# Matmul with row normalisation on one core: other slots for the left half of a group's result, the first streamed loads ahead of the identity matrix, and one finish moved a hook later

## The chip, the cores and the metric

The kernel runs on one core of a Trainium2 chip. The metric is the device time of one execution in microseconds (us), as the median of several runs; smaller is better. The span in a profile (first to last instruction) is about 1.8 us shorter than the device time of the same run.

Engines: PE is the tensor engine, DVE the vector engine, ACT the scalar engine, POOL the pool (GpSimd) engine, SP the engine that issues the stores and the transposing copies. "q" after an engine's name is its sequencer, which issues DMAs.

## The reference

```python
# a, b: 2048 x 2048 float32, gamma: 2048, eps = 1e-5
x = np.matmul(a, b)
rms = np.sqrt(np.mean(x ** 2, axis=-1, keepdims=True) + eps)
out = (gamma * x / rms).astype(np.float32)
```

## The kernel before

The output is made in 16 row blocks of 128 rows. Blocks 0 to 3 are made while `a` and `b` stream in (the "head"). Blocks 4 to 15 are made in six groups of two blocks, g = 2 to 7, each in two halves (j = 0: left 1024 columns, j = 1: right 1024 columns), with seven products in place of eight (Strassen-Winograd form). A product is eight matmuls of 128x128 by 128x512.

The result of one block and one half is kept in float32 in one of eight tiles ("slots"), `x_slot[0..7]`. In the profiles these are called x_95 to x_102. A slot is free again when the store of its old content has landed. Which slot a half gets is set in `x_tile`, in the order in which the halves are first asked for:

```python
def x_tile(mb, h):
    if (mb, h) not in x_half:
        n = n_x[0]
        n_x[0] += 1
        x_half[mb, h] = x_slot[n if n < 8 else (0, 4, 1, 5, 2, 6, 3, 7)[n % 8]]
    return x_half[mb, h]
```

Each group asks in the order: first block left, second block left, first block right, second block right. So with this map group 4 puts its second block's left half into slot 4, which held the second block of group 2.

The half of a group, cut to what matters. `at_hook(n)` runs other work at that place in the program; in the traces here each engine does its own instructions in program order.

```python
x11, x12, x21, x22 = (x_chunk(ra, c1), x_chunk(ra, c2), x_chunk(rb, c1), x_chunk(rb, c2))
t = x22                                            # in the second block's slot
at_hook(0)
product(g, j, 2, p2); nc.scalar.copy(out=t, in_=p2)   # ACT: first writer of the slot
last_squares(); at_hook(1)
product(g, j, 5, p5); nc.vector.tensor_tensor(out=t, in0=p5, in1=t, op=ALU.add)
at_hook(2)
product(g, j, 1, p1); # ... DVE: t = p1 - t
at_hook(3)
product(g, j, 4, p2, start=False)                  # adds onto p2: PE needs the copy above done
nc.scalar.copy(out=x21, in_=p2); square(rb, x21); # ... DVE: x11 = t + x21
at_hook(4)
product(g, j, 3, p5, start=False)
# ... cut: products 7 and 6, hooks 5 to 7
```

The work in the hooks for the left half of groups after the first (`nxt` is the first block of the next group):

```python
if g == G0 + 1:
    hook(2, finish, r3)            # group 3: block 3 is still to be finished
hook(0, row_factor, nxt)
hook(1, apply, nxt)                # ACT: 1.99 us, then a transposing copy on SP
hook(1, row_norm, nxt + 1)         # ACT: two squares of 1.06 us, a root
hook(3, row_factor, nxt + 1)
hook(3, finish, 2 * g - 2)         # first block of the group before
hook(4, apply, nxt + 1)
```

In the right half, `finish(2 * g - 1)` (second block of the group before) stands in hook 2, and in groups 2 to 5 POOL issues two loads of 1 MB in hook 0 (after that no loads are left). `finish` is: DVE sum, ACT root, DVE reciprocal, then twice a DVE scaling (1.28 us) and a store of 512 KB on SP.

Of the kernel before, what the change touches and what calls it, by code (L numbers as in the profile page):

```python
# [8 lines left out]
FP32 = mybir.dt.float32  # L9
BF16 = mybir.dt.bfloat16  # L10
# [7 lines left out]
def kernel(  # L18
# [13 lines left out]
    nc = tc.nc  # L32
    P = 128
    M, K = a.shape
    _, N = b.shape
# [4 lines left out]
    CH = 512  # L40
# [4 lines left out]
    G0 = HB // 2  # L45

    ctx.enter_context(tc.manual_schedule())
    consts = ctx.enter_context(tc.tile_pool(name="consts", bufs=1))
    a_pool = ctx.enter_context(tc.tile_pool(name="a_pool", bufs=2))
    sq_pool = ctx.enter_context(tc.tile_pool(name="sq_pool", bufs=1))  # L50
# [24 lines left out]
    x_slot = [consts.tile([P, HALF], FP32, name=f"x_{n}") for n in range(8)]  # L75
# [20 lines left out]
    def ah(kp):  # L96
        return ah_slot[(kp - 1) % NAH]

    def load_b(j, kp):
        nc.gpsimd.dma_start(  # L100
            out=raw[j][kp],
            in_=b[kp * W2:(kp + 1) * W2, j * HALF:(j + 1) * HALF].rearrange(
                "(t p) n -> p t n", p=P))

    def load_head(kp):
        nc.gpsimd.dma_start(  # L106
            out=ah(kp),
            in_=a[0:HB * P, kp * W2:(kp + 1) * W2].rearrange("(r p) k -> p r k", p=P))
        load_b(0, kp)
# [4 lines left out]
        a32[mb] = a_pool.tile([P, K], FP32, name="a32")  # L114
        nc.gpsimd.dma_start(out=a32[mb], in_=a[mb * P:(mb + 1) * P, :])

    identity_f = consts.tile([P, P], FP32, name="identity_f")
    make_identity(nc, identity_f)
    pace = consts.tile([P, 1], FP32, name="pace")

    def wait_for(src):

        nc.gpsimd.tensor_copy(out=pace, in_=src)

    for kp in range(1, 4):
        load_head(kp)
    identity = consts.tile([P, P], BF16, name="identity")
    nc.vector.tensor_copy(out=identity, in_=identity_f)
    identity_h = consts.tile([P, P], FP16, name="identity_h")
    nc.vector.tensor_copy(out=identity_h, in_=identity_f)  # L130


    warm = sq_pool.tile([P, 2 * CH], BF16, name="sq")
    nc.vector.memset(warm, 0.0)
    warm_bank = ps_a.tile([P, CH], FP32, name="acc")
    for _ in range(9):
        nc.tensor.matmul(warm_bank, warm[:, 0:P], warm[:, 0:CH], start=True, stop=True)

    gamma_sb = consts.tile([P, N], FP32, name="gamma_sb")
# [44 lines left out]
    def transpose_dma(mb):  # L184
        nc.sync.dma_start_transpose(at(mb), a16[mb])
# [39 lines left out]
    def row_apply(mb):  # L225
        a16[mb] = a16_slot(mb)
        if mb < HB + 2:
            nc.vector.tensor_scalar_mul(out=a16[mb], in0=a32.pop(mb), scalar1=factor.pop(mb))
        else:
            nc.scalar.activation(out=a16[mb], in_=a32.pop(mb), func=ACTF.Copy,  # L230
                                 scale=factor.pop(mb))
# [51 lines left out]
    x_half = {}  # L283
# [7 lines left out]
                             scale=inv_sqrt_n, accum_out=msq[mb][:, c:c + 1])  # L291

    def x_tile(mb, h):
        if (mb, h) not in x_half:
            n = n_x[0]
            n_x[0] += 1
            x_half[mb, h] = x_slot[n if n < 8 else (0, 4, 1, 5, 2, 6, 3, 7)[n % 8]]
        return x_half[mb, h]

    def x_chunk(mb, c):  # L300
        return x_tile(mb, c // 2)[:, (c % 2) * CH:(c % 2 + 1) * CH]
# [79 lines left out]
    for r in range(HB):  # L381
        x_tile(r, 0)
# [130 lines left out]
    def hooks_of(g, j):  # L513


        hooks = {n: [] for n in range(8)}
        nxt = 2 * g + 2

        def hook(n, work, *args):
            hooks[n].append(lambda: work(*args))  # L520

        def apply(mb):
            row_apply(mb)
            transpose_dma(mb)

        more = g + 1 < NG
        if j == 0:
            if g == G0:
                hook(0, row_factor, nxt)
                hook(1, row_norm, nxt + 1)  # L530
                hook(1, apply, nxt)
                hook(2, a_sums, g, (7, 6))
                hook(2, row_factor, nxt + 1)
                hook(2, finish, 1)
                hook(3, squares2, 2)
                hook(4, apply, nxt + 1)
                hook(4, finish, 2)
                hook(6, b_sum_7, 1, KP - 1)
            else:
                if g == G0 + 1:  # L540
                    hook(2, finish, r3)
                hook(0, row_factor, nxt)
                hook(1, apply, nxt)
                hook(1, row_norm, nxt + 1)
                hook(3, row_factor, nxt + 1)
                hook(3, finish, 2 * g - 2)
                hook(4, apply, nxt + 1)
        else:
            if g == G0:
                hook(1, squares2, r3)  # L550
                for kp in range(KP):
                    hook(2, b_sum_6, 1, kp)
            else:
                hook(2, finish, 2 * g - 1)
            if more:
                hook(3, a_sums, g + 1, (2, 5, 1))
                hook(6, a_sums, g + 1, (7,))
                hook(7, a_sums, g + 1, (6,))
            if g + 2 < NG:
                hook(0, load_after, g, nxt + 2)  # L560
                hook(0, load_block, nxt + 3)
                hook(5, row_norm, nxt + 2)
        return hooks

    def last_group():
# [4 lines left out]
        x11, x12, x21, x22 = ([x_chunk(mb, 2 * j + c) for j in range(2)]  # L570
                              for mb in (ra, rb) for c in range(2))
        xa, xb = x_tile(ra, 0), x_tile(rb, 0)
        gam = [gamma_sb[:, c * CH:(c + 1) * CH] for c in range(NCH)]
        gam_left = gamma_sb[:, 0:HALF]
# [98 lines left out]
    for g in range(G0, NG - 1):  # L673
        for j in range(2):
            group_half(g, j, hooks_of(g, j))
# [35 lines left out]
```

## Time and profile before

| | before |
|---|---|
| median (3 runs) | 229.66 us (229.09 to 230.08) |
| the profiled run | 227.94 us, span 226.2 us |
| PE busy | 211.3 us, 93% of the span |
| PE waits after the loading part | near 112, 126 and 150 us |

The page of the kernel before: its head, the row of busy times, and from the 40 slices the rows of PE (tenths busy), granted clock and DMA.

```profile
span 226.2 us, 3021 instructions
PE 211.3 (93%) x1041; PEld 98.3 (43%) x1041; DVE 161.7 (71%) x324; ACT 129.4 (57%) x272; POOL 24.5 (11%) x49
...
PE   5899999999999999999899699999999999999950
...
PEclk9999999999999999999999999999999999999997
DMA  5999999999972499808799059954798368244045
```

PE is the limit: full between the first two slices and the last two, but for one of 8 tenths (the 20th) and one of 6 (the 23rd, 124 to 130 us). In such a kernel only a matmul that starts late costs time. The matmuls there start 0.216 us apart, so I measure a loss as the start of a matmul, less the start of the one before, less 0.216 us. This is some 0.17 us more than the "idle before" that the timeline prints, because the modelled end of a matmul overlaps the next start.

The timeline of PE before, from 109 to 130 us, only the rows with a wait. Columns: start, length, engine, line, operation, count, and in brackets the idle time ahead and what ended it.

```profile
112.13 3.61 PE L278 MATMUL acc<-early,head_at 128*128 128x512 bf16 x16 [0.91 <-ACT x_102 L476]
...
126.19 3.61 PE L278 MATMUL acc<-t_left,at_even 128*128 128x512 bf16 x16 [1.81 <-ACT x_99 L476]
```

Both are product 4 waiting for the ACT copy of product 2 (line 476). What that copy waited for stands in the timeline of ACT before (first line), and the chain of waits before tells the rest (start, length, what).

```profile
125.56 0.59 ACT L476 COPY x_99<-acc 128x512 f32<-128x512 f32 x1 [3.00 <-DMA out_dram<-x_99]
```

```profile
114.14 1.29 DVE x_99 L323
...
115.45 10.00 DMA out_dram<-x_99
...
125.56 0.10 ACT x_99 L476
...
141.55 8.36 DMA out_dram<-x_101
...
150.01 0.59 ACT x_101 L476
...
150.65 1.46 PE acc L278 x6
```

The store of slot x_99 took 10.0 us to land and ACT stood idle 3.0 us for it; the same again with x_101 at 150 us. Most 512 KB stores of this kernel land in 2.6 to 3.1 us. These two go out while two loads of 1 MB are under way; DMA was busy for 0.85 and 0.98 of those two stretches. One comparison stands in the same trace: in group 6, where no loads are left to issue, the same finish in the same hook sends its two stores at 190 and 191 us. From the DMA view before, 183 to 195 us:

```profile
out_dram<-x_101 SPq DMA_DIRECT2D x1, 512.0 KB, 2.7
out_dram<-x_102 SPq DMA_DIRECT2D x1, 512.0 KB, 2.7
```

In groups 3, 4 and 5, beside loads, these stores take 8.4 to 10.0 us. This points to the loads but doesn't prove it.

### The profile page before, as it was taken

The numbers are of one execution on the slowest core, as the hardware profiler recorded it, in microseconds if no ns is written. First come the engines' busy times: TensorE is split into PE (matmuls) and PEld (weight loads), VectorE is DVE, ScalarE is ACT, GpSimd is POOL, SyncE is SP. The second block draws the span as 40 slices with busy tenths as digits, with TensorE's granted clock in tenths as the row PEclk, the third lists the DMA queues.
The fourth block names the chain that finished last, engine by engine and source line by source line (L and its number), as shares of the span: only waits on it lengthen the run. The fifth ranks groups of instructions, "written<-read, shape, count | busy, mean of one in ns | idle before, by whom it ended". The sixth has DMA issues, their size and how long they took to land.

```text
span 226.2 us, 3021 instructions
## 1 busy us (share of the span) xinstructions
PE 211.3 (93%) x1041; PEld 98.3 (43%) x1041; DVE 161.7 (71%) x324; ACT 129.4 (57%) x272; POOL 24.5 (11%) x49
## 2 busy tenths in 40 slices
PE   5899999999999999999899699999999999999950
PEld 2445454444454444444344344444444444444430
DVE  2426467983989989947988258962897289987692
ACT  2110003609698895792954788568956987334570
POOL 8433233200000002000010002000010000000000
PEclk9999999999999999999999999999999999999997
DMA  5999999999972499808799059954798368244045
GB/s 188 224 203 209 203 208 210 212 305 296 328 280 101 169 287 270 354 12 237 240 261 362 8 112 273 309 238 93 230 297 309 65 194 220 82 185 191 0 187 185
DMA packets 36176, 47.13 MB, mean 208 GB/s; under 512 B 21952, under 2 KB 26048, under 8 KB 34496
## 3 DMA queue, kind: packets, MB, share of 16 engines
q0 software_dynamic: 9648, 23.33, 41.4%
q1 hardware_dynamic: 26080, 22.29, 31.7%
q10 hardware_dynamic: 432, 1.31, 1.9%
q8 instruction: 8, 0.13, 0.2%
q14 instruction: 8, 0.07, 0.1%
HBM read 34.60 MB, written 16.78 MB: 227 GB/s over the span
## 4 chain that ended last, share of the span: by engine, by line
DMA 31%; PE 28%; issue 13%; ACT 13%; DVE 11%; POOL 2%; DVEq 0%; ACTq 0%; POOLq 0%
PE acc L278 28%; DMA a_428<-in_a_dram 8%; DMA b_6_83<-in_b_dram 7%; DMA b_2_79<-in_b_dram 5%; DMA out_dram<-x_99 4%; ACT sq L208 4%; DMA out_dram<-x_101 4%; ACT head_at L230 3%; ACT sq L290 3%; DMA a_863<-in_a_dram 2%; DVE early L253 1%; POOL early L106 1%; DVE x_101 L323 1%; DVE x_99 L323 1%; DVE x_98 L323 1%
## 5 line engine op out<-in xcount | busy, mean ns | idle before, releaser
L333 PEld LDWEIGHTS <-head_at 128*128 128x128 bf16 x240 | 22.9, 98 | 26.8 <-issue 1.3
L278 PEld LDWEIGHTS <-at_even 128*128 128x128 f16 x96 | 9.4, 98 | 13.4 <-issue 2.3
L278 PEld LDWEIGHTS <-head_at 128*128 128x128 f16 x96 | 9.4, 97 | 12.7 <-issue 1.6
L376 ACT COPY x_95<-acc 128x512 f32<-128x512 f32 x1 | 0.6, 586 | 24.1 <-PE acc L333 24.1
L278 PEld LDWEIGHTS <-s_105 128*128 128x128 f16 x96 | 9.4, 98 | 11.3
L278 PEld LDWEIGHTS <-s_103 128*128 128x128 f16 x96 | 9.4, 98 | 11.3
L278 PEld LDWEIGHTS <-s_107 128*128 128x128 f16 x96 | 9.4, 98 | 11.3
L278 PEld LDWEIGHTS <-s_104 128*128 128x128 f16 x96 | 9.4, 98 | 11.3
L278 PEld LDWEIGHTS <-s_106 128*128 128x128 f16 x88 | 8.6, 98 | 10.4
L216 DVE TENSOR_SCALAR s<-norm 128x1 f32<-128x1 f32 x12 | 1.8, 149 | 15.3 <-ACT norm L211 15.3
L278 PE MATMUL acc<-t_left,at_even 128*128 128x512 bf16 x48 | 10.8, 379 | 1.8 <-ACT x_99 L476 1.8
L278 PE MATMUL acc<-early,head_at 128*128 128x512 bf16 x48 | 10.8, 379 | 0.9 <-ACT x_102 L476 0.9
L278 PE MATMUL acc<-early,s_103 128*128 128x512 bf16 x48 | 11.3, 379 | 0.0
L278 PE MATMUL acc<-t_left,s_103 128*128 128x512 bf16 x48 | 11.3, 379 | 0.0
L278 PE MATMUL acc<-t_left,head_at 128*128 128x512 bf16 x48 | 10.8, 379 | 0.1
L278 PE MATMUL acc<-early,at_even 128*128 128x512 bf16 x48 | 10.8, 379 | 0.0
L371 DVE TENSOR_TENSOR x_98<-tbank,x_98 128x512 f32<-128x512 f32 x7 | 4.8, 692 | 7.6 <-PE tbank L365 7.6
L313 DVE RECIPROCAL r<-rms 128x1 f32<-128x1 f32 x16 | 2.6, 164 | 10.1 <-ACT rms L309 8.9
L169 DVE COPY head_at<-tbank 128x1024 bf16<-128x1024 bf16 x7 | 4.8, 691 | 6.6 <-PE tbank L164 6.6
L309 ACT ACTIVATE rms<-tot 128x1 f32<-128x1 f32 x14 | 2.7, 196 | 11.4 <-DVE tot L308 11.4
L290 ACT ACTIVATE sq<-x_97 128x512 bf16<-128x512 f32 x8 | 5.0, 628 | 3.5 <-DVE x_97 L591 3.0
L290 ACT ACTIVATE sq<-x_95 128x512 bf16<-128x512 f32 x8 | 5.0, 630 | 2.9 <-DVE x_95 L498 2.8
(366 smaller groups left out, 547.8 us busy)
## 6 DMA issues: line engine op xcount, KB each, us to landing
out_dram<-x_99 SPq DMA_DIRECT2D x4, 512.0 KB, 6.1
out_dram<-x_95 SPq DMA_DIRECT2D x4, 512.0 KB, 2.7
out_dram<-x_96 SPq DMA_DIRECT2D x4, 512.0 KB, 3.0
out_dram<-x_100 SPq DMA_DIRECT2D x4, 512.0 KB, 6.2
out_dram<-x_97 SPq DMA_DIRECT2D x4, 512.0 KB, 2.7
out_dram<-x_101 SPq DMA_DIRECT2D x4, 512.0 KB, 3.9
early<-in_a_dram POOLq DMA_DIRECT2D x7, 256.0 KB, 15.1
out_dram<-x_98 SPq DMA_DIRECT2D x3, 512.0 KB, 3.1
```

The lines of the kernel that those rows point to most:

```text
L106: nc.gpsimd.dma_start(out=ah(kp), in_=a[0:HB * P, kp * W2:(kp + 1) * W2].rearrange("(r p) k -> p r k", p=P))
L169: nc.vector.tensor_copy(out=head_at[:, 2 * kp:2 * kp + 2, :, :], in_=view)
L208: nc.scalar.activation(out=junk, in_=a32[mb][:, h * HALF:(h + 1) * HALF], func=ACTF.Square, scale=2.0 ** -8, accum_out=n2[:, h:h + 1])
L230: nc.scalar.activation(out=a16[mb], in_=a32.pop(mb), func=ACTF.Copy, scale=factor.pop(mb))
L253: nc.vector.tensor_tensor(out=sums[j][:, n, kp, :], in0=x, in1=y, op=op)
L278: nc.tensor.matmul(bank, lhsT[:, kp, :], rhs, start=(start and kp == 0), stop=(kp == KP - 1), skip_group_check=not start)
L290: nc.scalar.activation(out=sq[:, 0:CH], in_=src, func=ACTF.Square, scale=inv_sqrt_n, accum_out=msq[mb][:, c:c + 1])
L309: nc.scalar.activation(out=rms, in_=tot, func=ACTF.Sqrt)
L313: nc.vector.reciprocal(out=r, in_=rms)
L323: nc.vector.scalar_tensor_tensor(out=x, in0=x, scalar=r, in1=gamma_sb[:, h * HALF:(h + 1) * HALF], op0=ALU.mult, op1=ALU.mult)
L333: nc.tensor.matmul(bank, head_at[:, kt, r, :], head_rhs(c, kt), start=(kt == 0), stop=(kt == KT - 1))
L371: nc.vector.tensor_tensor(out=x, in0=part, in1=x, op=ALU.add)
```

## The change

Its intent: (1) the left half of a group goes into the two slots of the block that was stored *first*, two groups back, so that no copy waits for a late store; (2) the first streamed loads are issued before the identity matrix is made, and the warm-up of PE starts without waiting for the identity, with eleven matmuls in place of nine; (3) in group 3 the finish of the group before's first block moves one hook later.

```diff
+    load_head(1)
     identity_f = consts.tile([P, P], FP32, name="identity_f")
     make_identity(nc, identity_f)
-    for kp in range(1, 4):
+    for kp in range(2, 4):
         load_head(kp)
+    warm = sq_pool.tile([P, 2 * CH], BF16, name="sq")
+    nc.vector.memset(warm, 0.0)
     identity = consts.tile([P, P], BF16, name="identity")
     ...
-    warm = sq_pool.tile([P, 2 * CH], BF16, name="sq")
-    nc.vector.memset(warm, 0.0)
     warm_bank = ps_a.tile([P, CH], FP32, name="acc")
-    for _ in range(9):
+    for _ in range(11):
...
-            x_half[mb, h] = x_slot[n if n < 8 else (0, 4, 1, 5, 2, 6, 3, 7)[n % 8]]
+            if n < 8:
+                slot = n
+            else:
+                g = n // 4
+                slot = ((0, 4, 1, 5), (0, 1, 4, 5))[g // 2 % 2 == 0][n % 4] + 2 * (g % 2)
+            x_half[mb, h] = x_slot[slot]
...
-                hook(3, finish, 2 * g - 2)
+                hook(4 if g == G0 + 1 else 3, finish, 2 * g - 2)
```

More of the change, by code (lines that the diff above doesn't have):

```diff
@@ L115, in load_block @@
         nc.gpsimd.dma_start(out=a32[mb], in_=a[mb * P:(mb + 1) * P, :])
-    identity_f = consts.tile([P, P], FP32, name="identity_f")
-    make_identity(nc, identity_f)
     pace = consts.tile([P, 1], FP32, name="pace")
@@ L123, in wait_for @@
         nc.gpsimd.tensor_copy(out=pace, in_=src)
-    for kp in range(1, 4):
+    load_head(1)
+    identity_f = consts.tile([P, P], FP32, name="identity_f")
+    make_identity(nc, identity_f)
+    for kp in range(2, 4):
         load_head(kp)
+    warm = sq_pool.tile([P, 2 * CH], BF16, name="sq")
+    nc.vector.memset(warm, 0.0)
     identity = consts.tile([P, P], BF16, name="identity")
```

## The prediction

> **What bounds the kernel now.** The tensor engine. The page gives PE 211.3 us busy of a span of 226.2 us (93%), at full granted clock but at the end. From 12 us to 215 us matmuls start about 0.216 us apart (timeline of PE), so only a late matmul costs time. From successive starts I read these losses (a little larger than the view's "idle before", because modelled ends overlap the next start): 1.98 us at 126.2, 1.08 at 112.1, 0.29 at 150.7; in the loading part 0.51 at 11.5, 0.26 at 12.2, 0.56 at 24.5, 0.14 at 61.3, 0.47 at 67.0. The change doesn't touch the tail after 218 us.
>
> **Slots (the main part).** At 126.2 and 150.7 the chain of waits reads: PE, in groups 4 and 5, waits for the ScalarE copy of the first product; that copy waits for the store of the old x in the slot (x_99 issued 115.45, landed 125.48; x_101 issued 141.55, landed 149.9). The old content is the second row block of two groups back, stored in the middle of the following group beside two loads of 1 MB. The new map puts both left tiles of groups 4 and 5 into slots whose stores go out some 6 us earlier, and the right tiles, needed 14 us later, into the late ones. ScalarE was idle 3.0 and 1.75 us before these copies, so nothing else is known to hold them. Gain: 1.98 + 0.29 = 2.27 us, all on PE, hence on the critical path.
>
> **The moved finish.** In group 3 ScalarE sits 4.11 us in front of an rms (107.06) that waits for VectorE; the copy of product 4 (107.17), the 1.99 us apply and the copy at 111.5, for which PE waits 1.08 us, queue behind it. One hook later, that copy can go at about 102.9. But the rms still stands before the apply, and VectorE, busy with two 1.28 us scalings until 105.7, reaches its sum only at about 107.7. I work out the copy at 111.5 to be only 0.35 us earlier. Gain 0.3 us, at most 1.08.
>
> **The start.** The first two streamed loads are issued 0.7 us earlier (1.45 to 0.75), the identity is ready near 2.95 (needed at 6.36). Warm-up no longer waits for the identity: first matmul near 1.2 instead of 2.30, eleven end near 5.5; no time gained by itself. The Trainium skill ("TensorE: Matmul & The Clock Gate", the HAM clock gate) has the clock rise after some 3.4 us of work; the trace shows 0.43 us per matmul become 0.22 near 5.0 us. The loads gain only what DMA has free: the first streamed packets move at 6.5 us, while two queues of plain loads fill the DMA engines until 6. "DMA: Bandwidth & Descriptors" (Queues, rings and completion order) says engines take turns between queues; the trace shows hardly such mixing here, so the streamed bytes may start no earlier, or may delay the first a (landed 6.33). I expect 0.3 us gain at the waits at 12.2 and 24.5, between -0.3 and +0.7.
>
> **Sum.** 2.27 + 0.3 + 0.3 = 2.9 us: 229.66 becomes 226.8 us (-1.3%), range 225.7 to 228.3. Faster by over 2%: 0.05; within: 0.94; slower: 0.01.
>
> **What would show it.** No PE wait at product 4 of groups 4 and 5; ScalarE no longer waiting on a store; a rest of 0.5 to 0.9 us near 112; the wait for b_4 near 24 smaller. Wrong if: stores of the right half become late in their turn; group 4, now earlier, runs into its own loads or DMA transposes; the first a lands later than 6.6; or the wait near 112 vanishes or grows.

## The result, and the profile after

| | before | after |
|---|---|---|
| median, 4 runs each | 229.56 us (229.09 to 230.08) | 226.31 us (226.11 to 226.60) |
| the profiled run | 227.94 us, span 226.2 us | 226.60 us, span 224.8 us |

The ratio is 0.9859, 95% interval 0.9834 to 0.9884. Ratios here and below are the mean time of one kernel's fast runs over that of the other's of the same rounds, so not quite the ratio of the medians. The kernel is 3.25 us faster by the medians, 1.4%, clear of noise.

The two profiles differ by only 1.4 us of span. The profiled run of before, 227.94 us, was faster than each of its timed runs, so part of the gain can't be seen by laying these two traces side by side.

The page after, the same rows:

```profile
span 224.8 us, 3025 instructions
PE 212.1 (94%) x1043; PEld 98.6 (44%) x1043; DVE 161.8 (72%) x324; ACT 129.4 (58%) x272; POOL 24.5 (11%) x49
...
PE   7899999999999999999998999999999999999950
```

The timeline of PE after, 109 to 130 us, and below it that of ACT and of DVE after:

```profile
111.96 3.61 PE L279 MATMUL acc<-early,head_at 128*128 128x512 bf16 x16 [0.36 <-ACT x_102 L484]
...
119.98 0.39 PE L279 MATMUL acc<-b_0_77,s_104 128*128 128x512 bf16 x1 [0.96 <-DVE s_104 L244]
...
125.17 3.62 PE L279 MATMUL acc<-t_left,at_even 128*128 128x512 bf16 x16
```

```profile
124.12 0.57 ACT L484 COPY x_96<-acc 128x512 f32<-128x512 f32 x1
```

```profile
119.23 0.69 DVE L244 TENSOR_TENSOR s_104<-at_even 128x1024 f16<-128x1024 f16 x1 [1.96 <-DMA at_even<-head_at]
```

Product 4 of group 4 (now at 125.17) waits for nothing, and the copy before it, into x_96, doesn't either. But a new wait stands at 119.98: the first product of group 4 waits for a sum on DVE, and that for a transposing copy (`at_even`) that hadn't landed. The issues on the DMA view after, from 104 to 118 us (bytes, us from issue to landing), show that the late stores are as late as ever:

```profile
out_dram<-x_99 SPq DMA_DIRECT2D x1, 512.0 KB, 8.6
out_dram<-x_100 SPq DMA_DIRECT2D x1, 512.0 KB, 10.3
at_even<-head_at SPq DMA_TRANSPOSE x1, 7.7
```

So the stores did not get faster; nobody waits for them any more. The losses of PE in the two first traces, in us:

| where | before | after |
|---|---|---|
| start of product 4, second half of group 3 (112) | 1.08 | 0.53 |
| start of group 4 (120) | 0 | 1.12 |
| product 4 of group 4 (126) | 1.98 | 0 |
| product 4 of groups 5 and 6 (150, 175) | 0.36 | 0 |
| loading part, read at the transposes at 67: later by | | 0.37 |

0.37 - 0.55 + 1.12 - 1.98 - 0.36 = -1.40 us, which is the whole of the 1.38 us by which the last matmul came earlier (217.97 to 216.59).

### The profile page after: what moved, and what is told of

It reads as the page before. It is cut to its first block, busy times and chain, and to the rows that moved or that the text cites. A ratio compares the mean times of both kernels' runs of the same rounds, so it can differ in the third digit from the quotient of the medians.

```text
span 224.8 us, 3025 instructions
## 1 busy us (share of the span) xinstructions
PE 212.1 (94%) x1043; PEld 98.6 (44%) x1043; DVE 161.8 (72%) x324; ACT 129.4 (58%) x272; POOL 24.5 (11%) x49
## 3 DMA queue, kind: packets, MB, share of 16 engines
q10 hardware_dynamic: 432, 1.31, 2.0%
## 4 chain that ended last, share of the span: by engine, by line
PE 57%; DMA 14%; issue 12%; DVE 6%; ACT 5%; POOL 3%; DVEq 0%; ACTq 0%; POOLq 0%
PE acc L279 41%; PE acc L341 15%; DMA b_4_81<-in_b_dram 8%; DMA at_even<-head_at 3%; DMA a_865<-in_a_dram 2%; ACT sq L209 2%; ACT sq L291 1%; POOL early L106 1%; ACT head_at L231 1%; PE tbank L373 1%; PE tbank L165 1%; DVE x_95 L331 1%; DVE x_98 L331 1%; DVE x_96 L331 1%; DVE x_102 L331 1%
## 5 line engine op out<-in xcount | busy, mean ns | idle before, releaser
L279 PE MATMUL acc<-early,head_at 128*128 128x512 bf16 x48 | 10.8, 379 | 0.4 <-ACT x_102 L484 0.4
L279 PE MATMUL acc<-early,at_even 128*128 128x512 bf16 x48 | 10.8, 379 | 0.0
L279 PE MATMUL acc<-t_left,at_even 128*128 128x512 bf16 x48 | 10.8, 379 | 0.0
L279 PE MATMUL acc<-t_left,head_at 128*128 128x512 bf16 x48 | 10.8, 379 | 0.0
L291 ACT ACTIVATE sq<-x_97 128x512 bf16<-128x512 f32 x8 | 5.0, 628 | 3.5 <-DVE x_97 L599 3.0
L209 ACT ACTIVATE sq<-a_430 128x1024 bf16<-128x1024 f32 x2 | 2.1, 1058 | 7.5 <-DMA a_430<-in_a_dram 7.5
```

Source lines behind the costliest of these rows:

```text
L209: nc.scalar.activation(out=junk, in_=a32[mb][:, h * HALF:(h + 1) * HALF], func=ACTF.Square, scale=2.0 ** -8, accum_out=n2[:, h:h + 1])
L279: nc.tensor.matmul(bank, lhsT[:, kp, :], rhs, start=(start and kp == 0), stop=(kp == KP - 1), skip_group_check=not start)
L291: nc.scalar.activation(out=sq[:, 0:CH], in_=src, func=ACTF.Square, scale=inv_sqrt_n, accum_out=msq[mb][:, c:c + 1])
```

## The experiments

Theory after reading the two traces: the slots carry the gain, and more of it than the first trace of before shows; the moved finish costs more at 120 than it gains at 112; the start is worth nothing. Rivals: the missing 1.8 us are in the start; or the moved finish helps. Eleven runs were made, five rounds each (six runs with the profiled one), in three jobs of one chip each. The kernels of one job share eleven runs of before. All gave right results. In several of these traces about 20 of 1,041 matmul records are missing, which shows as a lone gap of 0.22 us about every 11 us; I leave those out. These traces also leave the numbers off the tiles' names (x for x_99).

| run | job | median, us | range | before in that job | ratio (95%) |
|---|---|---|---|---|---|
| before_again | 1 | 229.63 | 228.51 to 229.88 | 229.19 | 1.0012 (0.9980 to 1.0045) |
| slots_only | 1 | 225.95 | 225.57 to 226.27 | 229.19 | 0.9862 (0.9833 to 0.9890) |
| finish_only | 1 | 227.61 | 226.24 to 228.68 | 229.19 | 0.9939 (0.9898 to 0.9979) |
| start_only | 1 | 229.62 | 228.56 to 229.95 | 229.19 | 1.0017 (0.9986 to 1.0048) |
| slots_again | 2 | 225.77 | 225.56 to 226.10 | 229.05 | 0.9864 (0.9831 to 0.9898) |
| slots_finish | 2 | 226.47 | 226.12 to 226.80 | 229.05 | 0.9893 (0.9862 to 0.9924) |
| slots_finish_after | 2 | 225.86 | 225.76 to 226.49 | 229.05 | 0.9869 (0.9838 to 0.9900) |
| all_again | 2 | 226.28 | 225.92 to 226.92 | 229.05 | 0.9886 (0.9855 to 0.9918) |
| slots_split | 3 | 224.83 | 224.54 to 225.11 | 228.95 | 0.9861 (0.9823 to 0.9899) |
| slots_start_split | 3 | 224.88 | 224.74 to 225.39 | 228.95 | 0.9867 (0.9825 to 0.9910) |
| slots_pool_b | 3 | 226.19 | 226.02 to 226.46 | 228.95 | 0.9923 (0.9885 to 0.9961) |

The medians of before count all its runs; the ratios of job 3 leave out the five labelled slow.

The runs of before spread over 2.5, 2.5 and 4.4 us in the three jobs, those of every kernel with the new slots over 0.4 to 1.0 us. So within a job I compare the medians of the kernels with new slots directly with each other.

### before_again

No edit.

> The kernel before, unchanged, for a second trace of it. The median of its timed runs was 229.56 us, its first trace 227.94 us, the kernel after 226.31 us; the two traces differ by only 1.4 us of span. If the first trace caught a lucky execution, this one reads 229 to 230 us, and the wait for the old store near 126 us is then longer than 1.98 us, or the loading part loses about 1.5 us more than in the first trace. The first says that the slots are worth more than 2.3 us, the second that the start is where before loses. Ratio to before 1.000 within 0.3%.

Measured: 229.63 us; the profiled run 228.51 us. The timeline of PE, 110 to 180 us, rows with a wait:

```profile
112.47 3.61 PE L278 MATMUL acc<-early,head_at 128*128 128x512 bf16 x15 [0.83 <-ACT x L476]
...
125.86 3.61 PE L278 MATMUL acc<-t_left,at_even 128*128 128x512 bf16 x16 [1.15 <-ACT x L476]
...
150.89 3.61 PE L278 MATMUL acc<-t_left,head_at 128*128 128x512 bf16 x16 [0.70 <-ACT x L476]
...
175.44 3.61 PE L278 MATMUL acc<-t_left,at_even 128*128 128x512 bf16 x16 [0.22 <-ACT x L476]
```

The single wait at 126 is shorter here than in the first trace (a loss of 1.31 us), against what I expected of it, but those at 150 and 175 are longer (0.86 and 0.38). The three together: 2.34 us in the first trace, 2.55 us here, and 3.87 us (1.90 + 1.42 + 0.55) in start_only, which has the same slots. The wait for a store differs from one execution to the next, and it is not one place but groups 4, 5 and 6.

### slots_only

```diff
# before, plus:
-            x_half[mb, h] = x_slot[n if n < 8 else (0, 4, 1, 5, 2, 6, 3, 7)[n % 8]]
+            # ... the new map of the change
```

> Only the slot map. Theory: the waits at 126 and 150 us (1.98 and 0.29 us in the first trace) go and no new one comes, so about 2.3 us faster, 227.3 us, and with an unlucky store in before up to 3 us. The 1.08 us at 112 stay, the 1.12 us at 120 of the kernel after are not there, because the second transpose of group 3 is issued near 110.4 again. Rival (most of the gain is the start or the moved finish): less than 1.2 us.

Measured: 225.95 us, 3.24 us below before, and 3.28 us in the second job (slots_again). The timeline of PE, 110 to 180 us, has one row with a wait:

```profile
112.05 3.61 PE L278 MATMUL acc<-early,head_at 128*128 128x512 bf16 x15 [0.96 <-ACT x L481]
```

All three waits for stores are gone, and the 1.1 us at 120 of the kernel after are not there. The slots alone give the whole gain of the change. They also take away the scatter: the range of the runs falls from 2.5 us to 0.7 us, as it should if what varied was the landing of those stores. The rival that places the gain in the start is out.

### finish_only

```diff
# before, plus:
-                hook(3, finish, 2 * g - 2)
+                hook(4 if g == G0 + 1 else 3, finish, 2 * g - 2)
```

> Only the finish moved one hook later in group 3. Theory: the loss at 112 falls from 1.08 to about 0.5 us, the second transpose goes out 1 us later, behind the two stores, and the sums of group 4 wait for it: about 1.1 us lost at 120. What is lost at 120 shortens the wait at 126 by as much, as that waits for a store and not for PE. Sum: within 0.6 us of before. Rival (the move helps): 0.5 to 1 us faster.

Measured: 0.9939 (0.9898 to 0.9979), 1.4 us faster by the mean; more than I expected. The trace has the losses that I expected: 0.37 at 112, 1.41 at 120, none at 126, and 0.08 and 0.19 at 149 and 174. What is lost at 120 is thus taken off the wait at 126. The rest (shorter waits in groups 5 and 6) can't be told from the scatter of the store waits with one trace.

### start_only

```diff
# before, plus the first two hunks of the change (loads, identity, warm-up); slots and finish as before
```

> Only the start: first loads ahead of the identity, cleared tile first, eleven warm-up matmuls. The first trace of the kernel after has the first a landing 0.36 us later (6.69 instead of 6.33) and the eighth transpose at 67 us 0.37 us later. If that is the change's doing, 0.3 to 0.5 us slower than before. Rival (chance of one execution, or the gain that before's timed runs hide): no difference, or up to 1 us faster.

Measured: 1.0017 (0.9986 to 1.0048): no difference. The first real transpose starts at 6.42 us; in before 6.36 and 6.38. So the 6.72 of the first trace of the kernel after was chance; across all traces with the plain loads as they were it lies between 6.36 and 6.72, whichever start they have.

### slots_again, slots_finish, slots_finish_after, all_again

Four kernels on one chip. slots_again is slots_only. slots_finish is slots_only with the moved finish. all_again is the kernel after. slots_finish_after is slots_only with this edit:

```diff
-                hook(3, finish, 2 * g - 2)
+                if g != G0 + 1:
+                    hook(3, finish, 2 * g - 2)
                 hook(4, apply, nxt + 1)
+                if g == G0 + 1:
+                    hook(4, finish, 2 * g - 2)
```

> The slot map alone once more, as the partner on one chip for the three runs beside it. 225.5 to 226.3 us, spread of its runs under 1 us (the kernel before spread over 2.5 us); no loss but the 1.1 us near 112 between 70 and 215 us.

> Slot map and moved finish, start as before. Theory (the move gains 0.6 us at 112 and loses 1.1 us near 120, where nothing absorbs it any more): 0.3 to 0.7 us slower than slot map alone, with the second transpose of group 3 issued about 1 us later, behind the two stores, and the sums of group 4 waiting for it. Rival (the move stays a gain of its own, as it was without the new slots, where it made the kernel 1.4 us faster): 0.5 us or more faster than slot map alone.

> Slot map, and the finish of group 3 put behind the second apply in place of before it: scalar engine and store queue then meet the apply and its transpose first. If order in those two queues is what cost 1.1 us near 120, the transpose goes out by 110 us, the sums of group 4 wait no longer than in slot map alone, and the copy for which the tensor engine waits at 112 comes about 1 us earlier: loss there under 0.3 us. So 0.8 to 1.1 us faster than slot map alone, about 225.0 us. If instead the transposes are late for the traffic of the loads issued at 113 us, the loss near 120 stays and the kernel is no faster than slot map alone.

> The kernel after, on the same chip as the others. Theory: as slot map with moved finish, within 0.3 us, as the start is worth nothing; so about 0.5 us slower than slot map alone. Rival: the start costs the 0.36 us that its first trace shows, so it is 0.3 us or more slower than slot map with moved finish, and the first a lands again near 6.7 us.

Measured: 225.77, 226.47, 225.86 and 226.28 us. So with the new slots the moved finish makes the kernel 0.7 us slower, and the start changes it by -0.2 us, within the scatter of the runs. In this job the whole change is worth 2.77 us (229.05 to 226.28 us).

Why the move costs is seen on SP, which issues in program order in these traces. The timeline of SP, 98 to 118 us, of slots_again:

```profile
104.44 5.84 SPq L331 DMA_DIRECT2D out_dram<-x  x4
110.37 3.40 SPq L185 DMA_TRANSPOSE at_even<-head_at  x1
```

and of slots_finish:

```profile
104.68 6.44 SPq L331 DMA_DIRECT2D out_dram<-x  x4
111.21 3.34 SPq L185 DMA_TRANSPOSE at_even<-head_at  x1
```

The order in SP's queue is the same in both: the two stores of the finish stood ahead of the transposing copy before the move, too. What the move changes is DVE's order. There the finish now comes behind the sum `x11 = t + x21` (0.68 us), so its scalings start later, as the timelines of DVE of slots_again and of slots_finish show:

```profile
107.44 2.48 DVE L328 SCALAR_TENSOR_TENSOR x<-x,r,gamma_sb 128x1024 f32<-128x1024 f32 x2
```

```profile
108.28 2.48 DVE L328 SCALAR_TENSOR_TENSOR x<-x,r,gamma_sb 128x1024 f32<-128x1024 f32 x2
```

The second store waits for its scaling, and the copy behind it goes out 0.84 us later: 0.6 us from the sum put ahead, and 0.24 us because this trace was already that much behind when group 3 began. The copy also takes 7.9 us to land in place of 7.0; why is not shown. So the sums that need it are 1.75 us later, in the same two timelines:

```profile
117.37 1.90 DVE L243 TENSOR_TENSOR s<-at_even 128x1024 f16<-128x1024 f16 x3 [0.21 <-DMA at_even<-head_at]
```

```profile
119.12 1.90 DVE L243 TENSOR_TENSOR s<-at_even 128x1024 f16<-128x1024 f16 x3 [2.12 <-DMA at_even<-head_at]
```

In PE's losses: 1.02 at 112 without the move; 0.37 at 112 and 1.28 at 120 with it, a difference of 0.63 us, against 0.70 us measured in the medians.

slots_finish_after missed my expectation of 225.0 us. The copy does go out early (108.76) and lands in 4.3 us, and the loss at 120 is gone (what sets the time to land stays open: in slots_split, below, a copy issued at 108.75 us took 7.5 us), but the wait at 112 did not go: it moved to DVE and to product 3. The timeline of PE of that run:

```profile
113.99 1.89 PE L278 MATMUL acc<-early,head_at 128*128 128x512 bf16 x8 [1.08 <-DVE x L485]
```

In all three places tried, the two scalings of this finish (2.5 us) come soon after those of block 3 (2.5 us), and ACT's copy, the transposing copy or DVE's sum is late. My cure was aimed at the order in two queues; the trouble was two finishes in a row.

### slots_split, slots_start_split

In group 3, DVE is idle for 4.3 us ahead of the finish of block 3, as its root waits on ACT behind the apply and the squares. So I let the root go first and left the scalings where they were. slots_start_split has the start of the change as well.

```diff
# slots_only, plus:
+    early_r = {}
+    def early_rms(mb):
+        early_r[mb] = inverse_rms(mb)
     def finish(mb, order=(0, 1)):
-        r = inverse_rms(mb)
+        r = early_r.pop(mb) if mb in early_r else inverse_rms(mb)
...
                 if g == G0 + 1:
+                    hook(0, early_rms, r3)
                     hook(2, finish, r3)
```

> Slot map, and in group 3 the small part of the finish of row block 3 (sum, root, reciprocal) put at the start of the group, ahead of the 1.99 us apply and the 2.3 us of squares on the scalar engine; its two scalings stay where they were. Theory: the loss at 112 comes from the vector engine waiting 4.3 us for that root (idle until 102.9) and then having the scalings of two row blocks, 5 us, in a row. With the root early the scalings run in that idle time, the copies of product 4 and of the first product of the second half come 2 to 4 us earlier, the loss of 1.0 us at 112 goes and none takes its place: 0.9 to 1.1 us faster than slot map alone (225.8 to 226.0), so about 224.9 us. Rival (the two engines simply have too much work in this group, as putting the finish behind the apply only moved the wait): a wait of about 1 us comes back elsewhere in the group, time as slot map alone.

> As slots_split, with the start of the kernel after. Theory (the start is worth nothing): within 0.3 us of slots_split, first real transpose between 6.3 and 6.8 us as in all runs. Rival (the start helps or hurts by 0.4 us or more): a difference of that size between the two medians.

Measured: 224.83 and 224.88 us, as expected, and the fastest kernels: 0.9 to 1.1 us below slot map alone (225.77 and 225.95, in the other jobs), 1.5 us below the kernel after. The other jobs ran on other chips, so this is not a comparison on one chip. The ratio of this job, 0.9861, looks no better than that of slots_only, but it leaves out five of the eleven runs of before: at 229.77 to 230.77 us they are over 1.5% above the fastest (226.35 us) and so labelled slow, though their clock (0.98 to 0.99) is that of the others, and runs of 230.3 and 230.5 us count as fast in the other jobs. With all eleven (mean 229.04 us) the ratio is 0.9815, against 0.9856 for slots_only taken in the same way. Before scatters by the waits that these kernels no longer have, so its runs are a poor yardstick for half a per cent. The timelines of DVE around the finish of block 3, slots_again first, then slots_split:

```profile
102.92 0.16 DVE L318 RECIPROCAL r<-rms 128x1 f32<-128x1 f32 x1 [4.26 <-ACT rms L314]
103.12 2.48 DVE L328 SCALAR_TENSOR_TENSOR x<-x,r,gamma_sb 128x1024 f32<-128x1024 f32 x2
```

```profile
98.20 0.17 DVE L318 RECIPROCAL r<-rms 128x1 f32<-128x1 f32 x1 [0.27 <-ACT rms L314]
...
99.57 2.47 DVE L333 SCALAR_TENSOR_TENSOR x<-x,r,gamma_sb 128x1024 f32<-128x1024 f32 x2
```

The scalings run 3.5 us earlier, in time that was idle, and PE has no loss left between 68 and 215 us. The two medians differ by 0.05 us: with this, too, the start is worth nothing.

### slots_pool_b

```diff
# slots_only, plus:
     for t in range(2):
-        nc.scalar.dma_start(out=b0f[t], in_=b[t * P:(t + 1) * P, 0:HALF])
+        (nc.scalar, nc.gpsimd)[t].dma_start(out=b0f[t], in_=b[t * P:(t + 1) * P, 0:HALF])
```

> Slot map alone, but the second of the two plain loads of b is issued by the pool engine, ahead of the identity, in place of the scalar engine. In all traces so far the first byte of the pool engine's queue moves at 6.2 to 6.8 us, when the plain loads are nearly over, though the first of its loads is issued at about 1.3 us. If plain loads hold that queue back, it now starts at 4.5 to 5.5 us, as the plain loads are a third shorter (1 MB in place of 1.5 MB) and end near 5 us. If the queue has a start-up time of about 5 us of its own, its first byte still moves at 6.2 us or later, and the second b lands 1 to 2 us later than 8.5 us, which costs the tensor engine about that much.

Measured: 226.19 us, 0.2 to 0.4 us slower than slot map alone. The first byte of the POOL queue moved at 5.23 us; in the twelve other traces it was 6.2 to 6.8 us. The ACT queue's plain load ended at 4.74 us in place of 8.1 to 8.7 us. That is what one expects if plain loads hold the queue back. It is not shown: it is one trace, and the first load on the queue, issued at 1.25 us, was of another kind (no cast). A start-up time that is shorter for such a load (4.0 us here, against 5.0 to 5.4 us from issue to first byte) would look the same. It is not a gain: POOL makes the identity later, the tile for the warm-up is cleared after it, so the warm-up starts at 3.49 us in place of 2.30, and PE ran slow up to 9 us.

## Why the prediction was right or wrong

The time was right: 226.8 us predicted, 226.31 us measured, inside the range, and "within 2%". The sum of its terms was 2.9 us and 3.25 us came, but the terms are not those that came. That the total came out so close is in part luck: the slots were set about 1.0 us too low, the finish 1.0 us and the start about 0.3 us too high, and these errors nearly cancel.

- **Slots: mechanism right, size too small.** Predicted 2.27 us; slots_only measured 3.24 and slots_again 3.28 us. The figure was read off a single trace, of an execution that was faster (227.94 us) than all timed runs. The waits for stores came to 2.34, 2.55 and 3.87 us in three traces with the old slots. The sign of it was there to be read: a profiled run 1.1 us below the lowest timed run.
- **The slots' side conditions held.** No wait at product 4 of groups 4 and 5; the stores of the right half are as slow as before (8.6 and 10.3 us) and nothing waits for them.
- **Moved finish: wrong in sign.** Predicted 0.3 us gain; with the new slots it costs 0.7 us (with the old ones it came with a gain of 1.4 us, so the terms don't simply add). The first half of the reasoning held: the rest at 112 was predicted at 0.5 to 0.9 us and is 0.53 us in the kernel after (0.37 in slots_finish). What the sum left out is the SP queue: the two stores of the finish stand before the second transposing copy of the group, as they did, and with the scalings later on DVE that copy goes out 0.84 us later. The prediction named a collision of group 4 with its own transposes as a risk, but didn't count it. The failed step is "Gain 0.3 us, at most 1.08", which followed the ACT queue and not the SP queue.
- **Start: no gain.** Predicted 0.3 us (-0.3 to +0.7). start_only gives a ratio of 1.0017 (0.9986 to 1.0048). The step "the first two streamed loads are issued 0.7 us earlier" failed first: the first is issued at 1.25 us in place of 1.45 us, as POOL begins its first DMA 0.5 us later than it began the identity (0.74 us). The loads after the second go out 0.35 us later than before (the third at 3.38 us in place of 3.02), as the identity now stands ahead of them. And the streamed bytes begin at 6.2 to 6.8 us either way, as the prediction feared. Its warning sign "first a later than 6.6 us" fired in the first trace (6.69, the start of the first weight load that uses it, as the prediction's 6.33 was; the landing itself is 6.59, before 6.23), but that was chance; it did not in start_only and all_again.
- **Warm-up.** Predicted: first matmul near 1.2 us, the eleven end near 5.5 us. Measured 1.47 and 6.0 us. It gave no time, as said.

## What to carry to other kernels

When a buffer is reused, give the first writer the buffer whose store goes out first, not the one that comes next in a rotation: that took away 3.2 us and most of the scatter, while the slow stores stayed slow. Before moving work to another place in the program, follow every in-order queue that waits behind it, the DMA-issuing one too, and look for a small instruction (here a root of 0.2 us) that holds a long one back: sending just that one ahead gained 1 us where moving the whole piece lost 0.7 us. Look at two or three traces, or at least compare the profiled run with the timed ones, before sizing a wait for a DMA.

## What the Trainium skill lacked or had wrong

- "DMA: Bandwidth & Descriptors", section Queues, rings and completion order: it says that each DMA engine takes turns between the queues that have work, packet by packet. Here POOL's queue, whose first load is issued at 1.25 to 1.45 us, moved nothing until 6.2 to 6.8 us while 1.5 MB of plain loads ran on the two other queues (done at 8.1 to 8.7 us); with 1 MB on those it started at 5.23 us. The page doesn't tell of such a delay.
- The same page, section Anatomy of one DMA: its fit, 2.0 us + bytes / 436e3 (fitted on POOL's path), gives as an estimate 3.2 us for 512 KB. SP's stores come near it away from these loads (most 2.6 to 3.1 us) and not beside two loads of 1 MB (7.6 to 10.8 us); the page has no figure for that.
- "TensorE: Matmul & The Clock Gate", section Part 1: The HAM clock gate: it puts the rise of the clock about 4 us into sustained work, give or take 0.5 us. The traces show steps 2.9 us (before) and 4.2 us (after) after the first warm-up matmul, 0.43 to 0.22 us per matmul, and in slots_only the fp32 transposes were slow up to 7.7 us, 5.4 us after it. The page's remark that the window runs freely, and that the count of slow matmuls differs from run to run, fits that; its half microsecond does not.
- No page tells that POOL's first DMA begins 0.5 us later (1.25 us) than its first other instruction does in the same place (0.74 us).
